# Moving a channel shuffle's copies from two engines to VectorE alone, in program order

## The chip, the cores and the metric

The kernel runs on one core of a Trainium2 chip. Its metric is the device time of one execution in microseconds; medians of several executions are given with their range. The profile is of one execution, and its span runs from the first to the last instruction, about 1.7 us less than the time. No TensorE work exists here, and the granted clock is 1.0. Runs have a state, fast or slow: on one core, slow means over 1.5% above the fastest run of the same kernel. All runs quoted are fast unless the text says otherwise.

In lines of the profile, DVE is VectorE, ACT is ScalarE, POOL is GpSimd and SP is SyncE; SPq and ACTq are the streams that issue the DMA transfers. L49 is a line of the kernel's file, x22 a count, and "out_tile<-in_tile" reads as destination and source.

## The reference

```python
def reference(x, groups):                 # x: 16 x 64 x 64 x 256 float32, groups = 8
    batch, h, w, c = x.shape
    channels_per_group = c // groups      # 32
    x = x.reshape(batch, h, w, groups, channels_per_group)
    x = x.transpose(0, 1, 2, 4, 3)
    return x.reshape(batch, h, w, c).astype(np.float32)
```

Each block of 256 channels is permuted: seen as 8 rows of 32, it is transposed to 32 rows of 8. The input is 67.1 MB and so is the output, and nothing is computed.

## The kernel before

The tensor is cut into 21 tiles of 128 partitions x 24 blocks (24 KB a partition, 3.15 MB) and one of 8 blocks. Each is loaded contiguously, permuted within SBUF by strided copies, and stored contiguously. VectorE copies the first half of a tile and ScalarE the second. Loads are issued from SyncE's queue, stores from ScalarE's. Each side has four buffers.

```python
_SIZES = [24] * 21 + [8]
_IN_BUFS = 4
_OUT_BUFS = 4
_SHARES = (("vector", 1), ("scalar", 1))
# ... cut: flattening of x and out, the two pools, rows()
    def permute(engine, dst, src):
        src = src.rearrange("p (i g j) -> p i j g", g=G, j=CPG)
        dst = dst.rearrange("p (i j g) -> p i j g", j=CPG, g=G)
        # ... cut: scalar.copy or vector.tensor_copy, dst <- src

    for q in _SIZES:
        in_tile = in_pool.tile([P, biggest * c], F32, name="in_tile")
        nc.sync.dma_start(out=in_tile[:, : q * c], in_=rows(x_flat, first, q))
        out_tile = out_pool.tile([P, biggest * c], F32, name="out_tile")
        # ... cut: for each engine, permute its half of the columns
        nc.scalar.dma_start(out=rows(out_flat, first, q), in_=out_tile[:, : q * c])
        first += P * q
```

A scheduler orders the instructions of each engine. In this kernel it lets ScalarE, from the third tile on, run the copies of two tiles and then issue their two stores.

Of the kernel before, what the change touches and what calls it, by code (L numbers as in the profile page):

```python
# [1 line left out]

# [4 lines left out]


F32 = mybir.dt.float32
P = 128  # L10

_SIZES = [24] * 21 + [8]
_IN_BUFS = 4
_OUT_BUFS = 4

_SHARES = (("vector", 1), ("scalar", 1))


@with_exitstack
def kernel(  # L20
    ctx: ExitStack,
    tc: tile.TileContext,
    x: bass.AP,
    groups: bass.AP,
    out: bass.AP,
):
    nc = tc.nc
    b, h, w, c = x.shape
    G = int(groups)
    CPG = c // G  # L30
    assert G * CPG == c
    assert sum(_SIZES) * P == b * h * w
    biggest = max(_SIZES)

    x_flat = x.rearrange("b h w c -> (b h w c)")
    out_flat = out.rearrange("b h w c -> (b h w c)")

    in_pool = ctx.enter_context(tc.tile_pool(name="in_pool", bufs=_IN_BUFS))
    out_pool = ctx.enter_context(tc.tile_pool(name="out_pool", bufs=_OUT_BUFS))

    def rows(flat, first, q):

        return flat[first * c : (first + P * q) * c].rearrange("(p f) -> p f", p=P)

    def permute(engine, dst, src):
        src = src.rearrange("p (i g j) -> p i j g", g=G, j=CPG)
        dst = dst.rearrange("p (i j g) -> p i j g", j=CPG, g=G)
        if engine == "scalar":
            nc.scalar.copy(out=dst, in_=src)  # L49
        else:  # L50
            getattr(nc, engine).tensor_copy(out=dst, in_=src)  # L51

    first = 0
    for q in _SIZES:
        in_tile = in_pool.tile([P, biggest * c], F32, name="in_tile")
        nc.sync.dma_start(out=in_tile[:, : q * c], in_=rows(x_flat, first, q))
        out_tile = out_pool.tile([P, biggest * c], F32, name="out_tile")
        at, total = 0, sum(n for _, n in _SHARES)
        for k, (engine, n) in enumerate(_SHARES):
            last = k == len(_SHARES) - 1  # L60
            upto = q if last else min(q, at + -(-q * n // total))
            if upto > at:
                cols = slice(at * c, upto * c)
                permute(engine, out_tile[:, cols], in_tile[:, cols])
            at = upto
        nc.scalar.dma_start(out=rows(out_flat, first, q), in_=out_tile[:, : q * c])  # L66
        first += P * q


# [1 line left out]
_INS = ['x', 'groups']  # L71
_OUTS = [((16, 64, 64, 256), 'float32')]

_NUMBERS = {'groups': 8}


# [26 lines left out]
```

## Time and profile before

| | before |
|---|---|
| time, median of 3 | 317.7 us (317.62 to 317.93) |
| span of the profile | 316.0 us |
| DMA traffic | 134.2 MB, 425 GB/s over the span |
| DMA queues, share of 16 engines | 49.8% loads, 49.3% stores |
| VectorE, ScalarE busy | 21%, 38% |

Read it from the resource that is full. The sixteen DMA engines are taken 99% of the time and the copy engines far less, so the question for any change to the copies is whether it can make the DMA run dry, or fill a place where it does. The prediction below shows the lines and cuts the loss into stages.

### The profile page before, as it was taken

Reading aid. Unit: us, or ns where it says so; the run is one execution under the profiler, and the core shown is the slowest. Engines: PE = TensorE matmul, PEld = TensorE weight load, DVE = VectorE, ACT = ScalarE, POOL = GpSimd, SP = SyncE. Lnnn points to the kernel's source line nnn. Section 1 sums busy time; section 2 is a strip of 40 time slices with the busy share of each in tenths; the row PEclk is TensorE's granted clock in tenths of the full one; section 3 lists DMA queues with packets and bytes.
Section 4 is the critical chain, followed back from the end, with each engine's and each line's share of the span. In section 5 each row is a group of like instructions: output and inputs, shape, how many; then the busy total and the mean of one; then the engine's idle time right before and its main releaser. Section 6 shows DMA issues by size and latency. Waiting matters only on the chain.

```text
span 316.0 us, 236 instructions
## 1 busy us (share of the span) xinstructions
DVE 65.3 (21%) x22; ACT 118.9 (38%) x23; POOL 0.2 (0%) x4
## 2 busy tenths in 40 slices
DVE  0440321303030303113030303031220303030310
ACT  1681624425160606243351606061533426060620
POOL 0000000000000000000000000000000000000000
DMA  8999999999999999999999999999999999999996
GB/s 302 439 395 426 426 445 432 420 442 439 417 439 445 417 436 442 426 426 445 426 423 445 439 414 442 442 417 439 442 421 432 442 420 432 442 429 429 421 446 291
DMA packets 6337, 134.23 MB, mean 425 GB/s; under 512 B 704, under 2 KB 704, under 8 KB 704
## 3 DMA queue, kind: packets, MB, share of 16 engines
q1 hardware_dynamic: 3168, 67.11, 49.8%
q10 hardware_dynamic: 3168, 67.11, 49.3%
q14 instruction: 1, 0.01, 0.0%
HBM read 67.11 MB, written 67.11 MB: 425 GB/s over the span
## 4 chain that ended last, share of the span: by engine, by line
another core or an unknown queue 43%; DMA 32%; ACT 20%; ACTq 1%; issue 0%
DMA in_tile<-in_x_dram 32%; ACT out_tile L49 20%; ACTq L66 1%; ACTq L49 0%
## 5 line engine op out<-in xcount | busy, mean ns | idle before, releaser
L49 ACT COPY out_tile<-in_tile 128x3072 f32<-128x3072 f32 (+1 forms) x22 | 117.7, 5348 | 184.6 <-DMA in_tile<-in_x_dram 184.6
L51 DVE COPY out_tile<-in_tile 128x3072 f32<-128x3072 f32 (+1 forms) x22 | 65.3, 2968 | 238.3 <-DMA in_tile<-in_x_dram 238.3
L49 ACT ACT_TABLE_LOAD x1 | 1.3, 1283 | 0.7 <-PEq L84 0.7
L84 POOL MEMSET const-bfloat16-1.0<- 128x1 bf16 x1 | 0.1, 102 | 0.0
L84 POOL MEMSET const-uint8-127<- 128x1 uint8 x1 | 0.1, 102 | 0.0
L84 POOL MEMSET const-float32-1.0<- 128x1 f32 x1 | 0.1, 99 | 0.0
L84 POOL MEMSET const-float32-0.0<- 128x1 f32 x1 | 0.1, 98 | 0.2 <-issue 0.2
## 6 DMA issues: line engine op xcount, KB each, us to landing
in_tile<-in_x_dram SPq DMA_DIRECT2D x21, 3072.0 KB, 52.6
out_dram<-out_tile ACTq DMA_DIRECT2D x21, 3072.0 KB, 20.2
in_tile<-in_x_dram SPq DMA_DIRECT2D x1, 1024.0 KB, 47.9
out_dram<-out_tile ACTq DMA_DIRECT2D x1, 1024.0 KB, 10.4
```

Of the source, the lines that this page charges most:

```text
L49: nc.scalar.copy(out=dst, in_=src)
L51: getattr(nc, engine).tensor_copy(out=dst, in_=src)
L66: nc.scalar.dma_start(out=rows(out_flat, first, q), in_=out_tile[:, : q * c])
L84: nc = _bacc.Bacc("TRN2", target_bir_lowering=False, num_devices=1)
```

## The change

The intent is to take ScalarE out of the copying, so that its queue does nothing but issue stores, and to keep each engine's instructions in program order in place of the scheduler's order. The added line "manual_schedule" is what pins the order.

```diff
--- before.py
+++ after.py
@@ -12,8 +12,6 @@
 _SIZES = [24] * 21 + [8]
 _IN_BUFS = 4
 _OUT_BUFS = 4
-
-_SHARES = (("vector", 1), ("scalar", 1))
 
 
 @with_exitstack
@@ -42,27 +40,16 @@
 
         return flat[first * c : (first + P * q) * c].rearrange("(p f) -> p f", p=P)
 
-    def permute(engine, dst, src):
-        src = src.rearrange("p (i g j) -> p i j g", g=G, j=CPG)
-        dst = dst.rearrange("p (i j g) -> p i j g", j=CPG, g=G)
-        if engine == "scalar":
-            nc.scalar.copy(out=dst, in_=src)
-        else:
-            getattr(nc, engine).tensor_copy(out=dst, in_=src)
-
+    ctx.enter_context(tc.manual_schedule(engines=None))
     first = 0
     for q in _SIZES:
         in_tile = in_pool.tile([P, biggest * c], F32, name="in_tile")
         nc.sync.dma_start(out=in_tile[:, : q * c], in_=rows(x_flat, first, q))
         out_tile = out_pool.tile([P, biggest * c], F32, name="out_tile")
-        at, total = 0, sum(n for _, n in _SHARES)
-        for k, (engine, n) in enumerate(_SHARES):
-            last = k == len(_SHARES) - 1
-            upto = q if last else min(q, at + -(-q * n // total))
-            if upto > at:
-                cols = slice(at * c, upto * c)
-                permute(engine, out_tile[:, cols], in_tile[:, cols])
-            at = upto
+        nc.vector.tensor_copy(
+            out=out_tile[:, : q * c].rearrange("p (i j g) -> p i j g", j=CPG, g=G),
+            in_=in_tile[:, : q * c].rearrange("p (i g j) -> p i j g", g=G, j=CPG),
+        )
         nc.scalar.dma_start(out=rows(out_flat, first, q), in_=out_tile[:, : q * c])
         first += P * q
```

## The prediction

> **What bounds the kernel now.** I read the page first, its slices and queues, because a kernel that only copies must be bound by its transfers or by its copies.
>
> ```profile
> DVE 65.3 (21%) x22; ACT 118.9 (38%) x23; POOL 0.2 (0%) x4
> ...
> DMA  8999999999999999999999999999999999999996
> ...
> q1 hardware_dynamic: 3168, 67.11, 49.8%
> q10 hardware_dynamic: 3168, 67.11, 49.3%
> ```
>
> The copy engines are busy 21% and 38% of the span; the DMA row is at 9 (90% or more) in every slice but the first and the last, and the two queues, loads and stores, hold 49.8 + 49.3 = 99.1% of the sixteen DMA engines' time. The transfers are the bound. The view of waits says the same from the other side: both copy engines idle for loads and for nothing else.
>
> ```profile
> DVE out_tile L51 <- DMA in_tile<-in_x_dram: 238.3, 22, 11.6
> ACT out_tile L49 <- DMA in_tile<-in_x_dram: 184.6, 22, 9.2
> ```
>
> No copy waits for a store, that is, for an output buffer. Loads are also issued far ahead (the page's last part; the last number is the time to landing):
>
> ```profile
> in_tile<-in_x_dram SPq DMA_DIRECT2D x21, 3072.0 KB, 52.6
> ```
>
> Two loads in a row land 14.55 us apart (the copies that wait for them start at 103.62 and 118.17 us), so 52.6 us is 3.6 tiles of queue: a load waits some 38 us behind others before its own turn.
>
> I don't trust the chain of waits here: 43% of it is "another core or an unknown queue", on a program of one core. So I made a budget from the view by stages (columns: window, length, DVE, ACT and POOL busy with counts, clock, DMA share, GB/s).
>
> ```profile
> 0.00:4.00 4.00, 0.00 (x0) 1.28 (x1) 0.20 (x4) 1.00 0.63 184
> 4.00:18.30 14.30, 3.16 (x1) 5.73 (x1) 0.00 (x0) 1.00 1.02 438
> 18.30:31.00 12.70, 3.40 (x2) 6.02 (x2) 0.00 (x0) 1.00 1.00 404
> 31.00:161.00 130.00, 27.48 (x9) 49.65 (x9) 0.00 (x0) 1.00 1.00 433
> 161.00:292.00 131.00, 27.14 (x9) 48.89 (x9) 0.00 (x0) 1.00 1.00 432
> 292.00:302.40 10.40, 3.02 (x1) 5.48 (x2) 0.00 (x0) 1.00 1.02 436
> 302.40:314.00 11.60, 1.09 (x1) 1.89 (x1) 0.00 (x0) 1.00 0.94 403
> 314.00:316.00 2.00, 0.00 (x0) 0.00 (x0) 0.00 (x0) 1.00 0.01 4
> ```
>
> 134.22 MB at 432 GB/s take 310.7 us. The span is 316.0, so the whole loss is 5.3 us. By stage, loss = length x (432 - rate) / 432: 2.3 us before data flows, -0.2 to 18.3, 0.8 while the first stores begin, about -0.3 in the long middle, -0.1 to 302.4, 0.8 while the last stores run, 2.0 from the last data to the end; the sum is 5.3. Median time minus span is 1.7 us, which I carry over.
>
> [...]432 to 433 GB/s, loads and stores together, for 261 us[...]: with both queues full a 3.15 MB load lands every 14.55 us, and 2 x 3.146 MB / 14.55 us is 432 GB/s; the last load, 1.05 MB, lands 9.71 us after the one before it (copies at 292.64 and 302.35 us), the time of 1.05 + 3.15 MB at 432. [...]For five tiles between 103 and 176 us I read 429 to 437 GB/s during the copies and 431 to 434 between them, so copies don't slow the transfers. [...]here 3072 elements took about 3.02 us[...], so I use the trace's durations.
>
> **The change part by part.** It removes 22 ScalarE copies (117.7 us) and one table load (1.28 us, inside the 9 us in which nothing has landed yet). It gives VectorE the whole tile. It pins the program order, and this moves one more thing: the instruction order shows that, before, ScalarE's stream from the third tile on runs two copies and then two stores; now it holds 22 stores and no copy, each waiting for its own copy. Bytes, tile sizes, buffers and issuing queues stay.
>
> Length of the new copies, from the rows by form:
>
> ```profile
> L51 DVE COPY out_tile<-in_tile 128x3072 f32<-128x3072 f32 x21 | 64.2, 3058 | 231.6 <-DMA in_tile<-in_x_dram 231.6
> L51 DVE COPY out_tile<-in_tile 128x1024 f32<-128x1024 f32 x1 | 1.1, 1095 | 6.7 <-DMA in_tile<-in_x_dram 6.7
> ```
>
> The timeline shows 3.16 to 3.27 us for the first four copies and about 3.02 after. (3.02 - 1.095) / 2048 is 0.94 ns an element, which leaves about 0.13 us fixed. A 6144-element copy is then 5.91 us, the first four about 6.3, and the last of 2048 is 2.06. VectorE: 17 x 5.91 + 4 x 6.3 + 2.06 = 128 us, 40% of the span.
>
> *Middle.* The slower half of a tile took ScalarE 5.43 us; now it is 5.91. A load into a freed buffer is issued 0.5 us later, against some 38 us of queue: nothing. An output store of an even tile goes out 0.5 us later; that of an odd tile, which waited for the next tile's load (14.55 - 5.4, about 9.1 us), goes out that much earlier. As the DMA is full at 432 GB/s with the late stores, earlier ones find no gap to fill: 0.
>
> *Start.* The first store is issued near 17.4 instead of 16.80 us. Loads keep the DMA full meanwhile (438 GB/s): 0.
>
> *End.* This is the one place where order could pay.
>
> ```profile
> 292.64 5.43 ACT L49 COPY out_tile<-in_tile 128x3072 f32<-128x3072 f32 x1 [9.11 <-DMA in_tile<-in_x_dram]
> 302.35 1.94 ACT L49 COPY out_tile<-in_tile 128x1024 f32<-128x1024 f32 x1 [4.29 <-DMA in_tile<-in_x_dram]
> 302.41 2.25 ACTq L66 DMA_DIRECT2D out_dram<-out_tile  x2
> ```
>
> The copy of the last full tile ends at 298.07, but its store is issued at 302.41, behind ScalarE's wait for the last load. Changed, it goes out at about 292.6 + 5.9 = 298.6. What did the delay cost? After 302.4 the DMA moved 11.6 x 403 + 2 x 4 = 4.68 MB, while the last two stores are 4.19 MB: about 0.49 MB, 1.1 us, of the store before them was still under way. The first load, issued at 0.73 us, moved data by the window from 1 to 2 us (319 GB/s), so an issue needs about 1 us: the remainder covers it. Between 302.4 and 304.4 us the DMA still ran at 406 GB/s, a loss of 2 x 26 / 432 = 0.12 us. The gain is 0.1, at most 0.2 us. The last small store is ready at 302.35 + 2.06 + 0.4 = 304.8, while 3.15 MB are still going out: the longer last copy is hidden.
>
> Sum: 317.7 - 0.1 to 0.2 = 317.5 us, the same.
>
> **The rivals.** *Late stores cost more than it seems (faster).* Every other store is some 9 us late, the last large one 3.8 us. If the loss at both ends that could be tied to stores (0.8 + 0.8 us) vanished, the time would be 316.1. Against it: neither loss sits in the gap between copy and issue, since the rate at 302.4 is 406 and the lowest rates come after 311 us[...]. Even removing all 5.3 us would be 1.7%, under the 2% mark of 6.4 us. *VectorE becomes a bound, or holds buffers too long (slower).* It has one copy of 5.9 us in each 14.55 us; it would have to take over twice as long a copy before loads or stores went dry. If a copy of this form fell to half its rate (11.8 us), the middle would still be hidden, and the end grow by about nothing, for the last copy (4 us) still fits into the store before it: about 318. *The transfer rate itself changes,* because stores now stand in the queue continuously: a shift of 0.5% of the rate would be 1.6 us either way. The loads-only stretch (438), the mixed middle (432 to 433) and the stores-only end (424 from 304.4 to 311 us, my reading of a finer window) differ little, and the mix stays one to one.
>
> **Range and chances.** The three runs of before lie within 0.3 us. Taking 317.5 as centre, rival one reaches about 1.3 us down, rate and tail wobble about 0.9 us up; 316.5 to 318.3 should hold it 8 times in 10. Crossing 2% needs 6.4 us: faster would need more than all that is lost, slower a DMA that idles where it has three tiles queued. I give 1% to faster, 97% to same, 2% to slower.
>
> **What would show each step right or wrong.** The queues' share should stay near 99% and the middle at 432 to 433 GB/s. VectorE should show 21 copies of 5.9 to 6.3 us and one near 2.1, 128 us busy; ScalarE no busy time. VectorE should wait for loads alone, and a store should be issued within 0.1 us of its copy's end, every time. The last large store should go out near 298.6 and the window 302.4 to 304.4 be filled. The prediction is wrong if copies wait for stores, if landings of loads move off 14.55 us, or if the middle's rate shifts by more than 1%.

Passages that said of the hardware what no trace of this case shows are cut from it, at the places marked. The 0.4 us for the last small store (304.8 us) has no source; in the trace of the kernel before, issuing one store takes 0.34 to 0.38 us.

## The result, and the profile after

The changed kernel took **317.75 us** (median of 6, 317.28 to 318.0) and the kernel before, in the same rounds, 317.66 us (317.5 to 317.93). The ratio is 1.000, with a 95% interval of 0.9987 to 1.0013. A ratio here is the mean time of one kernel's fast runs over that of the other's of the same rounds, so it is not quite the ratio of the medians. The prediction was 317.5 us, within a range of 316.5 to 318.3.

The page of the changed kernel answers the first fence of the prediction (busy time by engine; the DMA row in 40 slices; the two queues).

```profile
DVE 121.7 (39%) x22; POOL 0.2 (0%) x4
...
DMA  8999999999999999999999999999999999999996
...
q1 hardware_dynamic: 3168, 67.11, 49.9%
q10 hardware_dynamic: 3168, 67.11, 49.3%
```

ScalarE's 118.9 us are gone and VectorE's 65.3 have become 121.7, yet the DMA row has not changed by a digit. The view of waits still has loads, and no store, in front of the copies:

```profile
DVE out_tile L49 <- DMA in_tile<-in_x_dram: 183.0, 22, 11.1
```

In the view by stages (window, length, VectorE and POOL busy, clock, DMA share, GB/s) each rate is within 6 GB/s of what it was, and within 2 GB/s in the lines shown:

```profile
18.30:31.00 12.70, 5.67 (x1) 0.00 (x0) 1.00 1.01 404
31.00:161.00 130.00, 51.25 (x9) 0.00 (x0) 1.00 1.00 433
161.00:292.00 131.00, 51.36 (x9) 0.00 (x0) 1.00 1.00 432
...
302.40:314.00 11.60, 2.02 (x1) 0.00 (x0) 1.00 0.94 405
```

The end differs in the way that was foreseen, in a size that does not matter. These are the same two microseconds of a finer view, the kernel before (which has a column for ScalarE) first:

```profile
302.40:304.40 2.00, 1.09 (x1) 1.89 (x1) 0.00 (x0) 1.00 0.95 406
```

```profile
302.40:304.40 2.00, 1.71 (x1) 0.00 (x0) 1.00 1.00 430
```

The timeline of the changed kernel shows why: the copy of the last full tile starts at 293.01 us, takes 5.69, and its store goes out at once.

```profile
298.73 0.34 ACTq L53 DMA_DIRECT2D out_dram<-out_tile  x1
```

That is 3.7 us earlier than before (302.41). It filled a loss of 0.12 us, which is below the spread of the runs. Ten of the stores were read one by one, and each is issued 0.02 to 0.04 us after its copy's end, as foreseen (within 0.1 us).

### The profile page after: what moved, and what is told of

Read it like the earlier page. It is cut to its first block, busy times and chain, and to the rows that moved or that the text cites. A ratio compares the mean times of both kernels' runs of the same rounds, so it can differ in the third digit from the quotient of the medians.

```text
span 316.0 us, 166 instructions
## 1 busy us (share of the span) xinstructions
DVE 121.7 (39%) x22; POOL 0.2 (0%) x4
## 4 chain that ended last, share of the span: by engine, by line
another core or an unknown queue 36%; DMA 32%; DVE 28%; issue 0%; DVEq 0%
DMA in_tile<-in_x_dram 32%; DVE out_tile L49 28%; DVEq L49 0%
## 5 line engine op out<-in xcount | busy, mean ns | idle before, releaser
L49 DVE COPY out_tile<-in_tile 128x6144 f32<-128x6144 f32 (+1 forms) x22 | 121.7, 5532 | 183.0 <-DMA in_tile<-in_x_dram 183.0
```

Source lines behind the costliest of these rows:

```text
L49: nc.vector.tensor_copy(out=out_tile[:, : q * c].rearrange("p (i j g) -> p i j g", j=CPG, g=G), in_=in_tile[:, : q * c].rearrange("p (i g ...
```

## The experiments

Twelve kernels were run, each beside the kernel before on the same chip. The rivals were: (A) the copies lie wholly beside the transfers; (B) the change joined a gain from order and a loss from the longer copy; (C) the copy or the late stores sit on the path. All kernels but the one without copies gave correct results.

### No copies at all

```diff
-_IN_BUFS = 4
+_IN_BUFS = 8
-        out_tile = ...; nc.vector.tensor_copy(...)
-        nc.scalar.dma_start(out=..., in_=out_tile[:, : q * c])
+        nc.scalar.dma_start(out=..., in_=in_tile[:, : q * c])
```

> No copies at all: each tile is stored straight from the tile it was loaded into (eight such tiles, as many bytes of buffer as before; the result is wrong on purpose). Theory (the transfers set the time and the copies lie wholly beside them): 316.8 to 317.8 us, VectorE and ScalarE with nothing to do, the middle still at 432 to 433 GB/s, load landings 14.5 us apart. Rival (copies cost something, by filling the ends or by disturbing the transfers, and the two kernels pay about the same): below 315 us, or a middle above 436 GB/s.

It took 317.46 us (317.16 to 317.88), ratio 0.9994 (0.9978 to 1.0011). A kernel that only moves the bytes is no faster, so no change to the copies could have gained more than the interval allows (0.2%). This is the strongest evidence for A, and it leaves nothing for a larger hidden gain. The view by stages also answers a question that the budget left:

```profile
4.00:18.30 14.30, 0.00 (x0) 1.00 1.01 412
18.30:31.00 12.70, 0.00 (x0) 1.00 1.00 432
31.00:161.00 130.00, 0.00 (x0) 1.00 1.00 433
```

Without a copy before it (5.71 us in the changed kernel) the first store can go out that much earlier, an estimate, as its issue was not read; and the dip that both kernels have between 18.3 and 31 us (404) moves into the window before it (412). So the dip is there without copying, and its place fits the first stores.

### The split copies in program order

```diff
+    ctx.enter_context(tc.manual_schedule(engines=None))
     first = 0
```

(on the kernel before)

> The kernel before with its split copies, and only the program order pinned, so that ScalarE issues each store before it waits for the next load. Theory (late stores meet a full DMA): 317.3 to 317.8 us, the last large store issued at about 298.1 us in place of 302.4, the rate from 302.4 to 304.4 us at 425 or more in place of 406. Rival (two effects cancelled in the change: order gained, the longer copy lost): 315 to 317.0 us. Also to see: whether the first four split copies are still longer (3.2 and 5.8 us) than the rest.

It took 317.59 us (317.50 to 317.68), ratio 0.9997 (0.9982 to 1.0012). The order alone moves the last large store to 298.22 us and the rate from 302.4 to 304.4 us to 442 GB/s, and the time not at all:

```profile
302.40:304.40 2.00, 1.14 (x1) 1.96 (x1) 0.00 (x0) 1.00 1.03 442
```

With this, rival B falls: within the interval (0.2%), there was no gain from order for the longer copy to eat.

### Stores held back on purpose

```diff
-        nc.vector.tensor_copy(<whole tile>)
-        nc.scalar.dma_start(<this tile>)
+        copy(nc.vector.tensor_copy, 0, q - 1)
+        copy(nc.scalar.copy, q - 1, q)
+        held.append((first, q, out_tile))
+        if len(held) > _LEAD:
+            store(*held.pop(0))
```

(on the changed kernel; _LEAD is 1 or 2, and the stores left over are issued after the loop)

> The changed kernel with 1 of the 24 column blocks of each tile copied on ScalarE, which takes that copy of the next tile before it issues a store: every store is held until the next load has landed, some 9 us after its copy ended. Theory: 317.3 to 318.2 us, the middle at 432 to 433 GB/s. Rival (a late store costs its delay): 22 stores times 9 us if nothing were hidden, and 326 us or more if even one in 20 of it showed.

> As the run before it, with stores held until the load after the next has landed, some 23 us after their copy. Theory: the loads run ahead into their four buffers meanwhile and the DMA stays full, so the middle stays at 432 to 433 GB/s; at the end the store before may be done when the last load lands, so that about one issue latency of 1 us shows: 317.5 to 319.5 us. Rival: above 322 us, with copies that wait for output buffers.

They took 317.60 us (317.44 to 317.77, ratio 0.9997, 0.9982 to 1.0012) and 317.86 us (317.45 to 317.88, ratio 1.0002, 0.9987 to 1.0017). A late store costs nothing that can be seen at either distance. But both runs mixed in something that I had not intended (the row by form of the second):

```profile
L49 DVE COPY out_tile<-in_tile 128x5888 f32<-128x5888 f32 x21 | 213.3, 10172 | 81.6 <-DMA in_tile<-in_x_dram 81.6
```

VectorE's copy of 23 blocks took 10.17 us, while its copy of 24 takes 5.70. In the run with one tile of lead the store was therefore held some 4 us after its copy, not 9. So I took two blocks for ScalarE in place of one:

> The run with stores held for two further loads, again, with 2 of the 24 blocks on ScalarE in place of 1. In the earlier run VectorE's copy of 23 blocks took 10.2 us where 24 blocks take 5.7, which mixed two changes; 22 is even. Expected if an odd number of blocks is what halved the rate: VectorE's large copies near 5.25 us, and 317.3 to 318.2 us with stores held some 22 us. Rival (any split makes the copy slow): 9.7 us. Rival for the time (the slow copies had hidden the cost of holding stores): above 320 us.

```profile
L49 DVE COPY out_tile<-in_tile 128x5632 f32<-128x5632 f32 x21 | 111.3, 5299 | 178.2 <-DMA in_tile<-in_x_dram 178.2
...
293.76 1.07 ACT L49 COPY out_tile<-in_tile 128x512 f32<-128x512 f32 x1 [8.69 <-DMA in_tile<-in_x_dram]
293.83 2.14 ACTq L45 DMA_DIRECT2D out_dram<-out_tile  x3
```

The large copy is 5.30 us, and the time 317.66 us (317.28 to 317.91), ratio 1.0003 (0.9988 to 1.0019), with every store of the middle some 24 us after its copy (two landings of 14.55 us less the 5.3 us of copying). The timeline lines show what happens to the delay: the loads run ahead, the last one lands near 293.7 us in place of 302.3, and the last three stores go out together while the DMA works through them. Nothing is lost: the same bytes move in another order, at 432 to 433 GB/s in the middle and 403 from 302.4 to 314 us, as in the kernel before. I had expected the end to show about 1 us of issue latency, up to 319.5 us; it shows none. The earlier pair stays useful by accident: a copy at half the rate, 10.2 us, does not change the time either.

### Longer copies

```diff
-        nc.vector.tensor_copy(...)
+        for _ in range(2):        # or 3
+            nc.vector.tensor_copy(...)
```

> The changed kernel with every copy made twice: 11.5 us of VectorE for a tile in place of 5.7, still under the 14.55 us that a tile's load and store take. Theory (copies have slack up to the transfer time of a tile): VectorE about 245 us busy, 317.3 to 318.5 us. Rival (the copy lies on a path, so that a longer one shows at least at the start and the end): 323 us or more, 5.7 us for one copy at one end.

> Every copy made three times: 17.2 us for a tile, over the 14.55 us. Theory: now VectorE is the bound. First landing 11.1 us + 21 x 17.2 + 6.1 for the small tile = 378 us, plus 3 to 5 us for the last store, plus 1.7 between span and time: 383 to 386 us, VectorE without a gap after the first landing, the DMA near 83% of full. Rival (slack is larger or smaller than a tile's transfer time): a time under 375 us.

Twice: 317.39 us (317.29 to 317.54), ratio 0.9998 (0.9981 to 1.0014), VectorE 242.3 us busy. Three times: 381.94 us (381.60 to 381.99), ratio 1.2027 (1.2009 to 1.2045). The page of the latter:

```profile
DVE 361.7 (95%) x66; POOL 0.2 (0%) x4
...
DMA packets 6337, 134.23 MB, mean 353 GB/s; under 512 B 704, under 2 KB 704, under 8 KB 704
```

The two together bracket the threshold: 2 x 5.68 = 11.4 us a tile is free, 3 x 5.68 = 17.0 us is paid in full, and 14.55 us, one tile's load and store, lies between. So with four load buffers and copies up to twice as long as they are, rival C falls too. 10.8 us of first load and 361.7 of copying make 372.5, with 1.5 us of small gaps 374.0, and the last stores bring the span to 380.1. I had expected 383 to 386 us; the time is 1 us below. The large copies took 355.7 us in place of the 361.2 that I had given them, and the gaps and a longer end (6.1 us after the last copy, in place of 3 to 5) took most of that back.

### Fewer buffers

```diff
-_IN_BUFS = 4
-_OUT_BUFS = 4
+_IN_BUFS = 2
+_OUT_BUFS = 2
```

(on the changed kernel and on the kernel before)

> The changed kernel with two buffers for loads and two for stores in place of four and four. A load is issued when the copy of two tiles earlier ends, a store when its own copy ends; a buffer's round of copy 5.7 us, some 3 us of latency and 14.5 us of shared transfer is 23 us, under two tiles' 29.1 us. Theory: 317.5 to 320 us, the same within 1%. Rival (four buffers are what hides the copy): above 324 us, with copies waiting for stores.

> The kernel before with two and two buffers. Its ScalarE still holds every other store behind the next tile's load, by up to 9 us. The same round becomes 23 + 9 = 32 us for every second tile, over the 29.1 us that two tiles take. Theory (the late stores are free only because of four buffers): slower than the vector-only kernel with two buffers, by about 3 us for each of ten pairs, 325 to 350 us, with copies waiting for stores. Rival (late stores are free in themselves): within 1% of the vector-only kernel with two buffers.

Both expectations missed. VectorE alone took 330.08 and 331.33 us, and in two further runs, which are put down as slow, 344.40 and 343.21. The split kernel took 323.71 and 326.38, and 330.54 and 330.21 in two runs put down as slow. The ratios to the kernel before with four buffers are 1.0415 (1.0392 to 1.0439, slower) and 1.0237 (1.0188 to 1.0286, unclear at the 2% mark). None of the slow runs shows a lower clock (1.0 in all), so the mark may only say how widely these two kernels scatter. So the kernel without late stores is not the better one with few buffers; by two fast runs of each it is slower by some 5 us. My theory for this pair, that late stores are free only thanks to four buffers, falls. In both, copies wait for stores (186.1 us on VectorE in the first, 181.3 on ScalarE in the second), so I asked which pool is short:

> The changed kernel with two load buffers and four store buffers. With two and two it lost 12 us and its copies waited for stores. Theory (the wait for a store's landing is what empties the load queue, so store buffers are what matters): copies wait for loads alone, 317.3 to 319 us. Rival (two load buffers are too few in themselves): above 323 us, with slices under 400 GB/s in the middle.

> The changed kernel with four load buffers and two store buffers. Copies will wait for stores, but four loads stand in the queue and keep the DMA full while they do: 317.3 to 320 us if a full load queue is enough. Rival (the store buffers were what cost in the kernel with two and two): 325 us or more. If both this run and the one with two load buffers stay near 318, it takes both pools being short for the DMA to run dry.

Two load buffers and four store buffers took 344.33 us (339.51 to 344.88, one of four runs slow), ratio 1.0792 (1.0729 to 1.0855). Four and two took 317.42 us (317.24 to 317.66), ratio 0.9996 (0.9982 to 1.0010), although its copies wait for stores:

```profile
DVE out_tile L49 <- DMA out_dram<-out_tile: 172.8, 20, 12.5
```

That wait is free, and the suspect that the waits named was the wrong one. What counts is the queue of loads. In the kernel with four and two (first line), a load takes 46.9 us from issue to landing, most of it behind other loads (a tile's load and store take 14.55 us); with two and four (second line) it takes 24.4:

```profile
in_tile<-in_x_dram SPq DMA_DIRECT2D x21, 3072.0 KB, 46.9
```

```profile
in_tile<-in_x_dram SPq DMA_DIRECT2D x21, 3072.0 KB, 24.4
```

The chain of the kernel with two and four (start, length, what) is a closed ring of load and copy:

```profile
18.04 5.76 DVE out_tile L49
23.79 0.02 issue
23.81 29.13 DMA in_tile<-in_x_dram
52.94 0.02 issue
52.96 5.71 DVE out_tile L49
58.67 0.02 issue
58.69 28.72 DMA in_tile<-in_x_dram
```

The end of a copy releases a load, that load's landing releases the copy two tiles later, and each round carries two tiles. 29.13 + 5.76 us is 34.9 us for a pair that the DMA could move in 29.1. With the median load of 24.4 us it is 30.1, still above 29.1. My expectation had put the round at 23 us; it counted a load's own transfer and forgot that it stands behind the load before it. (Its 3 us of latency agree with the start of the kernel before, by an estimate from the trace: the first load landed 10.28 us after its issue, and the second 7.28 us after the first, as the copies at 11.04 and 18.32 us show, which leaves 3.0.) By this ring a shorter copy would be worth its time here, which no run tests. With four load buffers it is not.

The ring does not cost at all times. In the kernel with two and two on VectorE alone, the copy two tiles later started 27.6 us (median) after a copy that ended from 20 to 110 us, and 23.4 us after one that ended from 180 to 290 us, so the load in between took no longer than that; 23.4 + 5.7 is no more than 29.1, and from 180 to 300 us that kernel moved 430 GB/s, with copies 14.54 us apart. It lost its time earlier (383 GB/s from 74 to 110 us) and at the end (279 GB/s from 312 us on). So two load buffers can keep nearly the full rate for a stretch; what lets a run settle into it is not shown.

Open is why two and four is slower than two and two, and why the split kernel did better than VectorE alone with two and two. The runs with two load buffers also differ among themselves by up to 14 us, and I have no run that tells these apart.

### Smaller tiles at both ends

```diff
-_SIZES = [24] * 21 + [8]
+_SIZES = [8, 16] + [24] * 19 + [16, 8, 4, 4]
```

> A try at a kernel that beats both: the changed kernel with tiles of 8 and 16 blocks first and 16, 8, 4 and 4 last, for the loss lies in the ends. Theory (the start is the latency of the first load and the end the receipt of the last store, and between them the DMA is full whatever the sizes): 316.8 to 317.8 us. Rival ([...]352 GB/s over the last 3 us[...]): 316 us or less.

This was the try at a kernel that beats both. It took 318.09 us (317.99 to 318.14), ratio 1.0016 (1.0004 to 1.0029): half a microsecond slower, a miss on both theories. The rate is measured, 352 GB/s from 311 to 314 us in the changed kernel. Of the theory's two ends, the first load of that kernel landed 10.31 us after its issue, and in the last 2.0 us of the span only 8 GB/s moved. The view by stages seems to put the loss at the end:

```profile
302.40:314.00 11.60, 2.53 (x3) 0.00 (x0) 1.00 0.91 382
314.00:316.00 2.00, 0.00 (x0) 0.00 (x0) 1.00 0.49 201
```

In the changed kernel these windows ran at 405 and 8, so most of the bytes only move later. Counted in bytes, most of the loss comes before: the first 31 us ran at 387 GB/s in place of 392, and at 302.4 us the kernel with small ends had 4.84 MB left to move, the changed one 4.71. By an estimate from these figures that is some 0.3 of the 0.4 us between the two profiled spans (316.4 and 316.0). No version was faster than the two kernels beyond the noise.

## Why the prediction was right

**The bound.** "The transfers are the bound" held: the time is that of a kernel with no copies at all, and the rate of each stage is within 6 GB/s of what it was.

**The middle.** The two zeros, for a load issued later and for stores issued earlier, are shown separately. Copies of 11.4 us a tile cost nothing, so 0.5 us more cannot; program order alone is worth nothing, and stores 24 us late cost nothing. The reason given, that a load stands three tiles back in the queue, is supported by the two runs with unequal pools: shortening the load queue costs 22 to 27 us (fast runs, 339.5 to 344.4 against 317.6), halving the store buffers costs nothing.

**The start.** The first store was issued at 16.80 us, as before, not at 17.4, because the first copy took 5.71 us. The term was zero either way.

**The end.** The store moved from 302.41 to 298.73 (298.6 foreseen), and the stretch filled from 406 to 430 GB/s. The gain of 0.1 to 0.2 us cannot be seen: the medians differ by 0.09 us the other way, inside the spread of either kernel. The close hit of the time is no evidence for this term.

**The size of the copies was a little off.** 5.91 us (6.3 for the first four) was foreseen, and all 21 took 5.66 to 5.75; VectorE was busy 121.7 us and not 128. The working scaled up copies that ran beside ScalarE's. From the rows of the changed kernel, (5.699 - 2.018) / 4096 is 0.90 ns an element and 0.18 us fixed, so 3072 elements alone would take 2.94 us (an estimate; no run copies that many on VectorE alone), where beside ScalarE they took about 3.02, and 3.16 to 3.27 in the first four tiles.

**What sets the rate of a copy was left open, without effect.** The prediction went on with the trace's durations. The run with 23 blocks shows a second rate, near half of the usual one (10.17 us / 5888 = 1.73 ns an element, against 5.30 / 5632 = 0.94 for 22 blocks; its last tile repeats it, 7 blocks in 3.18 us, where the changed kernel takes 2.02 for 8). So both kernels' copies already ran at the faster of the two rates that the runs show: VectorE's copies of 4, 6, 8, 12, 16, 22 and 24 blocks took 0.93 to 1.11 ns an element in the rows by form, those of 7 and 23 blocks 1.73 to 1.78. Why the two odd counts are slow is not shown. The rival "a copy at half its rate is still hidden" thereby got its own measurement.

**The rivals.** Late stores that cost more than they seem: excluded by the runs with program order and with held stores. (A slip without effect: from the centre, 317.5, down to this rival's 316.1 is 1.4 us and not 1.3.) VectorE as a bound: true only from somewhere between 11.4 and 17.0 us a tile on. A changed transfer rate: 432 to 433 GB/s in every kernel with four load buffers whose copies fit, held stores included.

## What to carry to other kernels

Where one resource is full from end to end, add up what it loses in each stage first: the sum (5.3 us here) caps every change that does not cut its work, and here the cap alone excluded a gain of 2%. Ask then how many requests stand in that resource's queue and what releases the next one; here slack in engines and order was free as long as the queue was not empty, and became time when the pool that feeds it got short. A large wait in the profile is not a cost by itself: 173 us of waiting for stores cost nothing, while the kernel that waited for loads alone, in a ring of two buffers, lost up to 27 us.

## What no run here tells

- What the stride costs. The strided copy, which reads with a step of 32 elements, took 2018 to 2050 ns for 2048 elements on VectorE. No run copies from a contiguous source.
- Why VectorE's copies of an odd number of blocks are slow. The outermost dimension was written as 23 on both sides, and the copy took 10.17 us against 5.30 for 22. What dimensions the compiled instruction carried cannot be seen in the profile.
- How VectorE and ScalarE copies between the same two SBUF tiles affect each other. In the kernel before, the first four pairs, which start within 0.01 us of each other, took 3.16 to 3.27 and 5.73 to 5.87 us; later pairs, mostly 0.04 to 0.2 us apart, took about 3.02 and 5.43. VectorE alone showed no longer first copies (5.67 to 5.72). Whether the common start or the first use of each buffer does it, no run here tells.
- How many load buffers suffice in general. Here four kept 432 GB/s, and two gave 323.7 to 344.4 us (fast runs) in place of 317.6, with times that vary from run to run; three were not tried.
